# A scale's chain in the order of a scheduled kernel: higher priority, two steps fewer, and one block's features on ScalarE

## The chip, the cores and the metric

The kernel runs on one core of a Trainium2 chip. The metric is the device time of one execution in microseconds (us). The core's engines run side by side, each through its own list of instructions in order: TensorE (PE in the profile), VectorE (DVE), ScalarE (ACT), GpSimd (POOL) and SyncE (SP), which here issues most DMAs. An instruction that needs a result of another engine waits for it, and all that stands behind it on its engine waits too.

## The reference

One layer of a diffusion backbone: attention and mLSTM heads side by side, a projection, and a SwiGLU feed-forward net (FFN). The FFN is what matters here:

```python
def swiglu(h, w_gu, w_down):
    g, u = jnp.split(h @ w_gu, 2, axis=-1)
    return (jax.nn.silu(g) * u) @ w_down

h2 = rmsnorm(x, norm2_w) * (1 + sc2) + sh2      # the FFN's features
x = x + g2 * swiglu(h2, w_gu, w_down)
```

The width is 1024 and the hidden width 2816, which is 22 slices of 128 for each of gate and up. There are 9 blocks of 128 tokens, taken as three chunks (0, 1, 2) of three blocks. All inputs and outputs are fp32.

## The kernel before, in words

**Chunk 0** goes through the FFN in fp32 with split operands: a value is held as a rounded high part and a low part (L175 casts the high part on ACT, L146 subtracts it from the whole on DVE or POOL), and each product takes three matmuls, high by high, high by low and low by high (L1220 to L1222 in the down projection, L1481 to L1483 in gate and up). While a slice of w_gu passes, ACT sums its squares into a column of `wsum` (L179, 44 columns).

**Chunks 1 and 2** go through the FFN together in fp16 parts, in "stage six", which replaces eight block products by seven (`pair6`, twelve matmuls each, L1651 to L1653). `weights6` makes its weight operands: it loads raw tiles of w_gu (L1625), adds them (S, L1629 to L1632), and splits them into fp16 tiles A with ACT (L1637) and DVE (L1638). Both need one power of two for w_gu, `six[:, 2:3]`. `features6` makes the other operand `Bt`, from transposed rows: a multiply-add for each of eight pieces of a block (F, L1593 on ACT and L1595 on DVE), differences T of two chunks (L1609 to L1612), and their splits (L1600 and L1616 on ACT, L146 on DVE).

**The power of two** comes from `weight_scale`: DVE takes the largest of the 44 sums (L1548), PE transposes the column, DVE takes the maximum (`pv`, L201), halves the exponent by a shift and an add on the bits (L203, L204, since these are squares), bounds it from below (L191), keeps the exponent's bits (L192) and makes the scale and its inverse (L193, L194). PE spreads the two numbers over the partitions by a matmul with a row of ones (L208), and DVE copies them to `six` (L209). `power_scale` is used for other scales too.

**Crossing from chunk 0 to stage six.** Chunk 0's last group holds five slices. Its down projection has two halves of the columns, n = 0 and n = 1, each with three blocks of 15 matmuls of 128x512. DVE gates a finished block out of its bank (t, L1209) and adds it to the row (L1210). In n = 0, block 0 goes first and then blocks 1 and 2 interleaved; `weight_scale` is called at the third step of n = 0 (`scaled_down`), `weights6(0)` behind the first step of n = 1.

**The order on each engine** is not the order of the code: a scheduler with a simulated timeline picks the next instruction by readiness and priority. `hot(n)` raises the priority of what is issued in it; `features6` runs under `hot(600)`. In stage six each step also passes a slice of w_down, loaded and summed for a later scale (`down_tally`: a 512 KB load at L1559, absolute values on ACT at L1561), 22 in all.

Of the kernel before, what the change touches and what calls it, by code (L numbers as in the profile page):

```python
# [12 lines left out]
I32 = mybir.dt.int32  # L13
AF = mybir.ActivationFunctionType
ALU = mybir.AluOpType
AX = mybir.AxisListType
# [15 lines left out]
NF = D_FF // P  # L32
EPS = 1e-6
CB = 3
# [16 lines left out]
def hybrid_step(ctx: ExitStack, tc: tile.TileContext, I: dict, O: dict):  # L51
    nc = tc.nc
    mm = nc.tensor.matmul
    act = nc.scalar.activation
    dve = nc.vector
# [4 lines left out]
    def hot(n):  # L60
        return tc.high_priority(n)

    def nm(s):
        uid[0] += 1
        return f"{s}_{uid[0]}"
# [10 lines left out]
    def emit(gen):  # L76
        for _ in gen:
            pass
# [31 lines left out]
    def bank():  # L110
        turn_of[0] += 1
        at = psum["mm"] if "mm1" not in psum or turn_of[0] % 4 else psum["mm1"]
        return at.tile([P, 512], F32, name=nm("mm"), tag="mm")
# [10 lines left out]
    def transpose(out, in_, n=P):  # L124
        nc.tensor.transpose(out, in_, ident[:n, :n])
# [19 lines left out]
    def sub(out, full, hi, eng):  # L145
        (dve if eng == "dve" else pool).tensor_tensor(out=out, in0=full, in1=hi, op=ALU.subtract)  # L146
# [38 lines left out]
    def behind(key):  # L185
        return tc.issue_after(loaded[key]) if key in loaded else nullcontext()

    def powers(v, n):

        v = v[0:n]  # L190
        dve.tensor_scalar(out=v[:, 0:1], in0=v[:, 0:1], scalar1=2.0 ** -16, scalar2=None, op0=ALU.max)  # L191
        dve.tensor_scalar(out=v[:, 1:2].bitcast(I32), in0=v[:, 0:1].bitcast(I32), scalar1=0x7F800000, scalar2=None, op0=ALU.bitwise_and)  # L192
        dve.tensor_scalar(out=v[:, 2:3].bitcast(I32), in0=v[:, 1:2].bitcast(I32), scalar1=-1, scalar2=266 * 2 ** 23, op0=ALU.mult, op1=ALU.add)  # L193
        dve.tensor_scalar(out=v[:, 3:4], in0=v[:, 1:2], scalar1=2.0 ** -12, scalar2=None, op0=ALU.mult)  # L194

    def power_scale(tp, one, bound, out, squares=False):

        ps = bank()
        transpose(ps[0:1, 0:P], bound)
        v = tp.tile([1, 4], F32, name=nm("pv"), tag="pv", bufs=2)  # L200
        dve.tensor_reduce(out=v[:, 0:1], in_=ps[0:1, 0:P], axis=AX.X, op=ALU.max)  # L201
        if squares:
            dve.tensor_scalar(out=v[:, 1:2].bitcast(I32), in0=v[:, 0:1].bitcast(I32), scalar1=1, scalar2=None, op0=ALU.logical_shift_right)  # L203
            dve.tensor_scalar(out=v[:, 0:1].bitcast(I32), in0=v[:, 1:2].bitcast(I32), scalar1=1, scalar2=0x1FC00000, op0=ALU.mult, op1=ALU.add)  # L204
        powers(v, 1)
        yield
        ps = bank()
        mm(ps[:, 0:2], one, v[:, 2:4], start=True, stop=True)  # L208
        dve.tensor_copy(out, ps[:, 0:2])  # L209
        yield  # L210
# [150 lines left out]
    for n in (1, 4):  # L361
        dve.tensor_scalar(out=bcol[:, n * KD : (n + 1) * KD], in0=bcol[:, n * KD : (n + 1) * KD],
                          scalar1=1.0, scalar2=None, op0=ALU.add)
# [839 lines left out]
    def t2():  # L1203
        return ft.tile([P, 512], F32, name=nm("t2"), tag="t2", bufs=nt2[0])
# [303 lines left out]
    def down(c, a, f0, nf, n):  # L1508
        g = gate_bc(1, n)
        acts = a["act"]  # L1510
        pieces = []
        for j in range(0, nf, 2):
            m = min(2, nf - j)
            rows = w_down[(f0 + j) * P : (f0 + j + m) * P, n * 512 : (n + 1) * 512].rearrange("(a p) n -> p a n", p=P)
            pieces.append(load_piece([(full_view, rows)], (m, 512)))
        yield from three_blocks(
            lambda k, i: (acts[k][0][:, i * P : (i + 1) * P], acts[k][1][:, i * P : (i + 1) * P]),
            pieces, nf, lambda i, ps: add_gated(a["x1"][i], ps, g(c * CB + i), n))
# [26 lines left out]

    def weight_scale():

        dve.tensor_reduce(out=six[:, 7:8], in_=wsum[:, 0 : 2 * NF], axis=AX.X, op=ALU.max)  # L1548
        emit(power_scale(fp, ones, six[:, 7:8], six[:, 2:4], squares=True))
        dve.tensor_tensor(out=six[:, 4:5], in0=six[:, 1:2], in1=six[:, 3:4], op=ALU.mult)  # L1550
        dve.tensor_tensor(out=six[:, 6:7], in0=six[:, 4:5], in1=six[:, 4:5], op=ALU.mult)
        dve.tensor_scalar(out=six[:, 5:6], in0=six[:, 4:5], scalar1=0.5, scalar2=None, op0=ALU.mult)

    def down_tally(j):

        loaded["n"] = (loaded["n"] + 1) % len(piece_tags)
        tag = piece_tags[loaded["n"]]
        raw = homes.get(tag, wp).tile([P, D], F32, name=nm("whi"), tag=tag, bufs=2)
        dma(raw, w_down[j * P : (j + 1) * P, :])  # L1559
        jk = ft.tile([P, D], BF16, name=nm("jk"), tag="t2", bufs=nt2[0])  # L1560
        act(jk, raw, AF.Abs, accum_out=wsum[:, 2 * NF + j : 2 * NF + j + 1])  # L1561

    def tallies():

        for j in range(NF):
            down_tally(j)
            yield

    def down_scale():

        n = NF
        dve.tensor_reduce(out=six[:, 7:8], in_=wsum[:, 2 * NF : 2 * NF + n], axis=AX.X, op=ALU.max)
        emit(power_scale(up, ones, six[:, 7:8], six[:, 8:10]))
        dve.scalar_tensor_tensor(out=six[:, 10:11], in0=six[:, 6:7], scalar=1.0 / DOWN_C, in1=six[:, 9:10], op0=ALU.mult, op1=ALU.mult)

    def features6(a, c, i, Bt, firsts):

        x1, r = a["x1"][i], a["rs"][i]
        at = slice(i * P, (i + 1) * P)
        F = a4p.tile([P, KD, P], F32, name=nm("F"), tag="A4", bufs=7)  # L1580
        wide = psum["S"].tile([P, 3, 512], F32, name=nm("S"), tag="S") if i % 2 == 0 else None
        for half in range(2):
            with hot(600):
                y = t2()
                act(y, x1[:, half * 512 : (half + 1) * 512], AF.Copy, scale=r)
                ps = wide[:, half] if i % 2 == 0 else psum["po"].tile([P, 512], F32, name=nm("po"), tag="po")
                for j in range(4):
                    transpose(ps[:, j * P : (j + 1) * P], y[:, j * P : (j + 1) * P])
                for j in range(4):
                    k = half * 4 + j  # L1590
                    s, t = mods6[:, k, 0:1], mods6[:, k, 1:2]
                    if j == 0:
                        act(F[:, k], ps[:, j * P : (j + 1) * P], AF.Identity, scale=s, bias=t)  # L1593
                    else:
                        dve.tensor_scalar(out=F[:, k], in0=ps[:, j * P : (j + 1) * P], scalar1=s, scalar2=t, op0=ALU.mult, op1=ALU.add)  # L1595
            yield
        for half, b in ((0, B11), (1, B21)) if c == 1 else ((1, B22),):
            v = F[:, half * 4 : half * 4 + 4]
            with hot(600):
                nc.scalar.copy(Bt[:, b, 0, :, at], v)  # L1600
                sub(Bt[:, b, 1, :, at], v, Bt[:, b, 0, :, at], "dve")
            yield
        if c == 1:
            firsts.append(F)
            return
        first = firsts.pop(0)
        T = sp.tile([P, 4, 4, P], F32, name=nm("T"), tag="S", bufs=1)
        with hot(600):
            dve.tensor_tensor(out=T[:, T1], in0=first[:, 0:4], in1=F[:, 0:4], op=ALU.subtract)  # L1609
            dve.tensor_tensor(out=T[:, T2], in0=F[:, 4:8], in1=T[:, T1], op=ALU.add)  # L1610
            dve.tensor_tensor(out=T[:, T3], in0=F[:, 0:4], in1=F[:, 4:8], op=ALU.subtract)
            dve.tensor_tensor(out=T[:, T4], in0=first[:, 4:8], in1=T[:, T2], op=ALU.subtract)  # L1612
        yield
        for j in (0, 2):
            with hot(600):
                nc.scalar.copy(Bt[:, j : j + 2, 0, :, at], T[:, j : j + 2])  # L1616
                sub(Bt[:, j : j + 2, 1, :, at], T[:, j : j + 2], Bt[:, j : j + 2, 0, :, at], "dve")
            yield
# [200 lines left out]
    sx = ctx.enter_context(tc.tile_pool(name="sx", bufs=1, reuse_waits="tile"))  # L1819
    six = sx.tile([P, 12], F32, name="six")  # L1820
    wsum = sx.tile([P, 4 * NF], F32, name="wsum")
    mods6 = sx.tile([P, KD, 2], F32, name="mods6")
    ones = sx.tile([1, P], F32, name="ones")
    dve.memset(ones, 1.0)
# [55 lines left out]
    def late_rows():  # L1880
        rows_back(o_d[CB:], lambda: mixing(a4p, "A4", 7), late, 700)
        yield

    feats = chain(late_rows(), *[features6(nxt, 1, i, Bt, firsts) for i in range(CB)],
                  [None], attn_out(far, g_d[0, 1], late), *[features6(far, 2, i, Bt, firsts) for i in range(CB)])

    def scaled_down():
        for i, units in enumerate(down(0, cur, *GROUPS[-1], 0)):
            if i == 3:
                weight_scale()  # L1890
            yield units

    main = chain(groups(0, cur, GROUPS[NG:-1]), gate_up(cur, *GROUPS[-1]), scaled_down())
# [95 lines left out]
```

## Time and profile before

| | |
|---|---|
| three runs | 1494.35, 1494.94 (median), 3020.9 us |
| the profiled execution | 1496.35 us, of which the span of instructions is 1494.6 |
| PE busy | 1410.6 us, 94% of the span |
| DVE busy | 1103.5 us, 74% |
| ACT busy | 873.7 us, 58% |
| mean granted PE clock | 0.983 |

Times in the profile count from the start of its span. In rows of the timeline stand the start, the duration, the engine, the line, the operation with its tiles (out <- in), and in brackets the time for which the engine had been idle and what released it. Rows of the windows give, for a stretch, each engine's busy time (with instructions), the granted PE clock, the DMA engines' share and the rate. Matmul rows overlap, since the next starts before the last has drained.

### The profile page before, as it was taken

The page shows a single profiled execution, that of the slowest core. Times are in us where ns is not written, and L with a number is a line of the kernel's source. Part 1 is how long each engine was busy: PE and PEld are TensorE (multiplying, and loading weights), DVE is VectorE, ACT ScalarE, POOL GpSimd, SP SyncE. Part 2 cuts the span into 40 slices and gives each one's busy share as a digit, 9 for nine tenths or more (in the row PEclk, how much of TensorE's full clock was granted, in tenths as well). Part 3 has the DMA queues.
Part 4 walks back from the last instruction along what each step waited for, and adds up shares of the span by engine and source line. Part 5 has one row for each costly group of instructions (what it writes and reads, how often), then busy time and mean ns, then how long its engine had stood idle before and what let it go on. Part 6 is the DMA issues. An engine that isn't in the chain of part 4 may idle for free.

```text
span 1494.6 us, 22805 instructions
## 1 busy us (share of the span) xinstructions
PE 1410.6 (94%) x8285; PEld 989.5 (66%) x8285; DVE 1103.5 (74%) x2240; ACT 873.7 (58%) x1613; POOL 218.1 (15%) x310
## 2 busy tenths in 40 slices
PE   6899999998899889999999999998999999999996
PEld 3644667666677667888999997974645654654552
DVE  4878556775777988667687758788976877786667
ACT  4854477865857745464776754849642642463254
POOL 0113422232222435410100010000000000000000
PEclk9799999999999999999999999999999999999998
DMA  9565323753558865666757764459231321232112
GB/s 369 171 201 189 95 75 65 145 94 67 93 106 167 202 216 149 172 201 172 202 154 174 183 148 146 141 193 348 85 107 43 101 83 43 71 113 70 44 43 85
DMA packets 256166, 206.46 MB, mean 138 GB/s; under 512 B 167022, under 2 KB 208198, under 8 KB 256054
## 3 DMA queue, kind: packets, MB, share of 16 engines
q1 hardware_dynamic: 253054, 199.00, 47.9%
q10 hardware_dynamic: 2872, 5.62, 1.1%
q8 instruction: 65, 1.06, 0.3%
q14 instruction: 47, 0.39, 0.1%
q0 software_dynamic: 128, 0.39, 0.1%
HBM read 153.38 MB, written 13.26 MB: 111 GB/s over the span
## 4 chain that ended last, share of the span: by engine, by line
PE 54%; DVE 7%; DMA 3%; ACT 3%; issue 1%; POOL 0%; SPq 0%; ACTq 0%; DVEq 0%; POOLq 0%
PE mm L1653 6%; PE mm L1651 6%; PE mm L1652 6%; PE mm L1735 3%; PE mm L1736 3%; PE mm L1737 3%; PE mm L1482 3%; PE mm L1483 3%; PE mm L1481 3%; PE S L1132 2%; PE mm L1221 2%; PE mm L1220 2%; PE mm L1222 2%; PE mm L1256 2%; PE mm L1258 1%
## 5 line engine op out<-in xcount | busy, mean ns | idle before, releaser
L1651 PE MATMUL mm<-Bt,A 128*128 128x384 f16 x616 | 198.2, 326 | 2.8 <-ACT A L1637 1.3
L1652 PE MATMUL mm<-Bt,A 128*128 128x384 f16 x616 | 200.8, 326 | 0.0
L1653 PE MATMUL mm<-Bt,A 128*128 128x384 f16 x616 | 198.0, 326 | 1.7 <-DVE A L1638 1.7
L175 ACT CAST whi<-raw 128x1024 fp32r<-128x1024 f32 (+1 forms) x78 | 79.5, 1024 | 78.1 <-PE mm L1221 27.5
L1139 DVE SCALAR_TENSOR_TENSOR pl<-pr,st,ph 128x1152 f16<-128x1152 f32 (+1 forms) x72 | 97.9, 1360 | 36.6 <-ACT ph L1138 36.6
L146 DVE TENSOR_TENSOR wlo<-raw,whi 128x1024 fp32r<-128x1024 f32 (+1 forms) x78 | 93.3, 1197 | 41.6 <-ACT whi L175 37.8
L1481 PE MATMUL mm<-aTh,whi 128*128 128x384 f32 x352 | 119.2, 339 | 0.0
L1483 PE MATMUL mm<-aTh,wlo 128*128 128x384 f32 x352 | 119.0, 339 | 0.0
L1482 PE MATMUL mm<-aTl,whi 128*128 128x384 f32 x352 | 118.9, 338 | 0.0
L1135 ACT ACTIVATE pr<-S,st 128x1152 f32<-128x1152 f32 (+1 forms) x72 | 81.6, 1133 | 56.4 <-DVE st L1134 55.2
L1134 DVE TENSOR_REDUCE st<-S 128x1 f32<-128x1152 f32 (+1 forms) x72 | 88.9, 1234 | 25.2 <-PE S L1132 25.1
L530 PE MATMUL wi<-headw,hT 128*128 128x384 f16 x288 | 94.5, 328 | 1.2 <-ACT th L820 1.2
L531 PE MATMUL wi<-headw,hT 128*128 128x384 f16 x288 | 94.5, 328 | 0.0
L532 PE MATMUL wi<-headw,hT 128*128 128x384 f16 x288 | 94.4, 328 | 0.0
L1132 PE MATMUL S<-kst,qT 128*128 128x384 f32 (+1 forms) x400 | 87.6, 349 | 4.0 <-ACT pr L1135 4.0
L1138 ACT ACTIVATE ph<-pr,st 128x1152 f16<-128x1152 f32 (+1 forms) x72 | 83.7, 1163 | 12.7 <-DVE st L1137 5.3
L1651 PEld LDWEIGHTS <-A 128*128 128x128 f16 x616 | 60.2, 98 | 42.8 <-ACT A L1637 2.8
L1653 PEld LDWEIGHTS <-A 128*128 128x128 f16 x616 | 60.3, 98 | 42.2 <-DVE A L1638 2.5
L1652 PEld LDWEIGHTS <-A 128*128 128x128 f16 x616 | 60.3, 98 | 42.1 <-issue 2.6
L1132 PEld LDWEIGHTS S<-kst,qT 128*128 128x128 f32 x400 | 69.4, 189 | 7.8 <-ACT pr L1135 5.4
L146 POOL TENSOR_TENSOR hl<-tn,hl 128x384 fp32r<-128x384 f32 x22 | 28.9, 1314 | 313.2 <-ACT hl L1504 297.8
L1637 ACT ACTIVATE A<-S,six 128x1024 f16<-128x1024 f32 x44 | 49.0, 1141 | 37.3 <-PE mm L1653 19.7
(478 smaller groups left out, 3724.3 us busy)
## 6 DMA issues: line engine op xcount, KB each, us to landing
raw<-in_w_gu_dram SPq DMA_DIRECT2D x88, 512.0 KB, 3.6
raw<-in_w_down_dram SPq DMA_DIRECT2D x42, 512.0 KB, 3.9
a<-in_w_ada_dram SPq DMA_DIRECT2D x24, 512.0 KB, 6.4
whi<-in_w_down_dram SPq DMA_DIRECT2D x22, 512.0 KB, 8.6
iraw<-in_w_in_dram SPq DMA_DIRECT2D x32, 256.0 KB, 3.3
x<-in_x_sample_dram SPq DMA_DIRECT2D x11, 512.0 KB, 5.7
raw<-in_w_out_dram SPq DMA_DIRECT2D x10, 512.0 KB, 3.7
aw<-in_w_ada_dram SPq DMA_DIRECT2D x8, 512.0 KB, 5.4
```

Source lines behind the costliest of these rows:

```text
L146: (dve if eng == "dve" else pool).tensor_tensor(out=out, in0=full, in1=hi, op=ALU.subtract)
L530: mm(ps[:, :n], ah, wh[:, k % 2, c0 : c0 + n], start=(k == 0), stop=False)
L531: mm(ps[:, :n], ah, wl[:, k % 2, c0 : c0 + n], start=False, stop=False)
L532: mm(ps[:, :n], al, wh[:, k % 2, c0 : c0 + n], start=False, stop=(k == KD - 1))
L1132: mm(S[:, n, 0:w], qT[:, h, :], kst[kv][:, t, c0 + n * w : c0 + (n + 1) * w], start=(t == 0), stop=(t == 1))
L1139: dve.scalar_tensor_tensor(out=plv, in0=prv, scalar=st[:, 3:4], in1=phv, op0=ALU.mult, op1=ALU.subtract)
L1481: mm(ps, wh[:, k, :], th[:, k, :], start=(k == 0), stop=False)
L1482: mm(ps, wh[:, k, :], tl[:, k, :], start=False, stop=False)
L1483: mm(ps, wl[:, k, :], th[:, k, :], start=False, stop=(k == KD - 1))
L1651: mm(ps, wh[:, k], bt[:, 0, k], start=first and k == 0, stop=False, skip_group_check=True)
L1652: mm(ps, wh[:, k], bt[:, 1, k], start=False, stop=False, skip_group_check=True)
L1653: mm(ps, wl[:, k], bt[:, 0, k], start=False, stop=k == 3, skip_group_check=True)
```

## The change

1. `weight_scale()` is called under `hot(900)`.
2. For squares, the shift and the add on bits become one multiply-add: 0.5 times the number that the bits form, plus 0x1FC00000. The lower bound L191 is left out for this call; a constant column of 2^-32 in `wsum` takes its place, which is set at the start, so that w_down's columns move by one. The chain has five DVE steps from `pv` to the scale instead of seven.
3. In `features6`, all eight multiply-adds of the last block of chunk 2 go to ACT; before, two of the eight did.

```diff
-    def powers(v, n):
+    def powers(v, n, least=True):
         v = v[0:n]
-        dve.tensor_scalar(out=v[:, 0:1], in0=v[:, 0:1], scalar1=2.0 ** -16, scalar2=None, op0=ALU.max)
+        if least:
+            dve.tensor_scalar(out=v[:, 0:1], in0=v[:, 0:1], scalar1=2.0 ** -16, scalar2=None, op0=ALU.max)
...
         if squares:
-            dve.tensor_scalar(out=v[:, 1:2].bitcast(I32), in0=v[:, 0:1].bitcast(I32), scalar1=1, scalar2=None, op0=ALU.logical_shift_right)
-            dve.tensor_scalar(out=v[:, 0:1].bitcast(I32), in0=v[:, 1:2].bitcast(I32), scalar1=1, scalar2=0x1FC00000, op0=ALU.mult, op1=ALU.add)
-        powers(v, 1)
+            dve.tensor_scalar(out=v[:, 0:1].bitcast(I32), in0=v[:, 0:1].bitcast(I32), scalar1=0.5, scalar2=0x1FC00000, op0=ALU.mult, op1=ALU.add)
+        powers(v, 1, not squares)
...
     def weight_scale():
-        dve.tensor_reduce(out=six[:, 7:8], in_=wsum[:, 0 : 2 * NF], axis=AX.X, op=ALU.max)
+        dve.tensor_reduce(out=six[:, 7:8], in_=wsum[:, 0 : 2 * NF + 1], axis=AX.X, op=ALU.max)
...
-                    if j == 0:
+                    if j == 0 or (c, i) == (2, CB - 1):
                         act(F[:, k], ps[:, j * P : (j + 1) * P], AF.Identity, scale=s, bias=t)
...
+    dve.memset(wsum[:, 2 * NF : 2 * NF + 1], 2.0 ** -32)
...
             if i == 3:
-                weight_scale()
+                with hot(900):
+                    weight_scale()
```

In the order of the changed kernel, lines from L192 to L204 of before stand one lower in number (L193 for L192 and so on; its L204 is the new multiply-add).

**VectorE, at the end of half n = 0.** Before, from the second gating of n = 0 to the end of the chain (`pv`):

```order
L1209 TENSOR_TENSOR t_2204_11204<-mm_11155,gl_8050 128x512
L1209 TENSOR_TENSOR t_2205_11207<-mm_11156,gl_8050 128x512
L1612 TENSOR_TENSOR T_11100<-F_10317,T_11100 128x512
L191 TENSOR_SCALAR pv_11172<-pv_11172 1x1
L1210 TENSOR_TENSOR x1a<-x1a,t_2198_11152 128x512
L146 TENSOR_TENSOR Bt<-T_11100,Bt 128x2x4x128
L1210 TENSOR_TENSOR x1a<-x1a,t_2204_11204 128x512
L1210 TENSOR_TENSOR x1a<-x1a,t_2205_11207 128x512
L192 TENSOR_SCALAR pv_11172<-pv_11172 1x1
L146 TENSOR_TENSOR Bt<-T_11100,Bt 128x2x4x128
L193 TENSOR_SCALAR pv_11172<-pv_11172 1x1
L194 TENSOR_SCALAR pv_11172<-pv_11172 1x1
```

And the same place after the change, from the new multiply-add on:

```order
L204 TENSOR_SCALAR pv_11173<-pv_11173 1x1
L146 TENSOR_TENSOR wlo_11225<-raw_11223,whi_11224 128x512
L1612 TENSOR_TENSOR T_11101<-F_10318,T_11101 128x512
L193 TENSOR_SCALAR pv_11173<-pv_11173 1x1
L146 TENSOR_TENSOR Bt<-T_11101,Bt 128x2x4x128
L194 TENSOR_SCALAR pv_11173<-pv_11173 1x1
L195 TENSOR_SCALAR pv_11173<-pv_11173 1x1
L1209 TENSOR_TENSOR t_2198_11153<-mm_11133,gx_11113 128x512
L1209 TENSOR_TENSOR t_2204_11203<-mm_11156,gl_8051 128x512
L1209 TENSOR_TENSOR t_2205_11206<-mm_11157,gl_8051 128x512
L146 TENSOR_TENSOR Bt<-T_11101,Bt 128x2x4x128
L209 COPY six<-mm_11179 128x2
```

The whole chain now stands ahead of the three gatings of n = 0, with one large Bt subtraction in front of its end and the other behind the gatings.

**TensorE, between the halves.** Before, L208 stands behind the first block of n = 1 (mm_11270), which itself follows the last matmul of n = 0:

```order
L1222 MATMUL mm_11270<-whi_11219,hl_11019 128x512
L1220 MATMUL mm_11270<-whi_11225,hl_11109 128x512
L1221 MATMUL mm_11270<-wlo_11226,hl_11109 128x512
L1222 MATMUL mm_11270<-whi_11225,hl_11109 128x512
L208 MATMUL mm_11180<-pv_11172,ones 128x2
L1220 MATMUL mm_11230<-whi_11213,hl_10743 128x512
L1221 MATMUL mm_11230<-wlo_11214,hl_10743 128x512
```

After, it follows the last matmul of n = 0 (mm_11133, mm_11156, mm_11157 are that half's blocks):

```order
L1222 MATMUL mm_11133<-whi_11128,hl_11110 128x512
L1222 MATMUL mm_11156<-whi_11128,hl_11110 128x512
L1222 MATMUL mm_11157<-whi_11128,hl_11110 128x512
L208 MATMUL mm_11179<-pv_11173,ones 128x2
L1220 MATMUL mm_11229<-whi_11212,hl_10744 128x512
L1221 MATMUL mm_11229<-wlo_11213,hl_10744 128x512
L1222 MATMUL mm_11229<-whi_11212,hl_10744 128x512
```

All 45 matmuls of n = 1 now stand behind L208; before, 15 of them stood ahead of it.

**SyncE, the loads at the start of stage six.** Before (raw_11481 and raw_11483 are the weights of slice 1 of stage six, raw_11678 belongs to slice 2; whi are slices of w_down to be summed):

```order
L1525 DMA fw_11520<-in_final_norm_w_dram 128x512
L1625 DMA raw_11678<-in_w_gu_dram 128x1024
L1525 DMA fw_11522<-in_final_norm_w_dram 128x512
L1559 DMA whi_11393<-in_w_down_dram 128x1024
L1559 DMA whi_11477<-in_w_down_dram 128x1024
L1625 DMA raw_11481<-in_w_gu_dram 128x1024
L1625 DMA raw_11483<-in_w_gu_dram 128x1024
L1559 DMA whi_11413<-in_w_down_dram 128x1024
```

After:

```order
L1525 DMA fw_11519<-in_final_norm_w_dram 128x512
L1559 DMA whi_11392<-in_w_down_dram 128x1024
L1559 DMA whi_11476<-in_w_down_dram 128x1024
L1525 DMA fw_11521<-in_final_norm_w_dram 128x512
L1625 DMA raw_11480<-in_w_gu_dram 128x1024
L1625 DMA raw_11482<-in_w_gu_dram 128x1024
L1625 DMA raw_11677<-in_w_gu_dram 128x1024
L1559 DMA whi_11412<-in_w_down_dram 128x1024
```

The two slices of w_down now stand ahead of every raw weight tile listed here, and slice 1's tiles ahead of slice 2's first one. On ScalarE the eight features of the last block stand in groups of four, three and one (before, single ones in two places), all of them ahead of the 128x512 cast of the last weight piece of n = 1 (L175), as the two did before. GpSimd's list is the same in both kernels, and the order on the other engines up to some 20 us before this place too, apart from the new memset.

More of the change, by code (lines that the diff above doesn't have):

```diff
@@ L1560, in down_tally @@
         jk = ft.tile([P, D], BF16, name=nm("jk"), tag="t2", bufs=nt2[0])
-        act(jk, raw, AF.Abs, accum_out=wsum[:, 2 * NF + j : 2 * NF + j + 1])
+        act(jk, raw, AF.Abs, accum_out=wsum[:, 2 * NF + 1 + j : 2 * NF + j + 2])
     def tallies():
@@ L1571, in down_scale @@
         n = NF
-        dve.tensor_reduce(out=six[:, 7:8], in_=wsum[:, 2 * NF : 2 * NF + n], axis=AX.X, op=ALU.max)
+        dve.tensor_reduce(out=six[:, 7:8], in_=wsum[:, 2 * NF + 1 : 2 * NF + 1 + n], axis=AX.X, op=ALU.max)
         emit(power_scale(up, ones, six[:, 7:8], six[:, 8:10]))
```

## The prediction

> **What bounds the kernel now.** The page's first part shows the engine with most work, and a window query cuts the end of the run into stretches. Columns of a window: PE, its weight loads, DVE, ACT and POOL busy (instructions), granted PE clock, DMA share, GB/s.
>
> ```profile
> PE 1410.6 (94%) x8285; PEld 989.5 (66%) x8285; DVE 1103.5 (74%) x2240; ACT 873.7 (58%) x1613; POOL 218.1 (15%) x310
> 974.00:996.00 22.00, 19.34 (x91) 15.71 (x90) 21.30 (x41) 8.35 (x12) 2.47 (x1) 1.00 0.54 198
> 996.00:1002.40 6.40, 6.40 (x29) 5.02 (x27) 6.17 (x13) 5.11 (x6) 0.00 (x0) 1.00 0.44 116
> 1002.40:1036.00 33.60, 29.10 (x171) 16.03 (x171) 25.55 (x48) 28.31 (x48) 0.00 (x0) 1.00 0.98 367
> 1036.00:1475.00 439.00, 438.99 (x2450) 239.60 (x2449) 327.04 (x496) 198.48 (x256) 0.00 (x0) 1.00 0.23 76
> ```
>
> PE is the engine that sets the time. From 1036 to 1475 it has no gap (438.99 of 439.00), so whatever is won ahead of 1036 reaches the end as it is, and nothing that another engine does in those 439 us can give it back or add to it, short of opening a gap. Where the change acts, PE idles twice: 2.66 us in 974 to 996 (22.00 less 19.34) and 4.50 us in 1002.4 to 1036. In the first of these DVE is full (21.30 of 22.00) and ACT is not (8.35); in the second DMA is full (0.98). At most 2.66 + 4.50 = 7.16 us are to be had.
>
> The timeline of PE shows the single gaps: the first two in the crossing, the others in the first 33 us of stage six.
>
> ```profile
> 987.76 0.86 PE L1222 MATMUL mm<-whi,hl 128*128 128x512 f32 x3
> 990.14 0.50 PE L1220 MATMUL mm<-whi,hl 128*128 128x512 f32 x1 [1.51 <-DVE t L1209]
> 995.05 0.38 PE L208 MATMUL mm<-pv,ones 1*128 1x2 f32 x2 [1.15 <-DVE pv L194]
> 995.36 0.50 PE L1220 MATMUL mm<-whi,hl 128*128 128x512 f32 x1
> 1002.44 0.34 PE L1651 MATMUL mm<-Bt,A 128*128 128x384 f16 x1
> 1014.80 0.32 PE L1651 MATMUL mm<-Bt,A 128*128 128x384 f16 x1 [0.40 <-DVE u L1670]
> 1020.26 0.34 PE L1653 MATMUL mm<-Bt,A 128*128 128x384 f16 x1 [0.82 <-DVE A L1638]
> 1027.65 0.34 PE L1653 MATMUL mm<-Bt,A 128*128 128x384 f16 x1 [0.90 <-DVE A L1638]
> 1034.86 0.32 PE L1651 MATMUL mm<-Bt,A 128*128 128x384 f16 x1 [0.67 <-DVE u L1670]
> ```
>
> Half n = 0 ends at 988.62 (987.76 + 0.86). PE then waits 1.51 us for a bank that DVE gates out, and 1.15 us for the scale chain's last step.
>
> **The change, part by part.** DVE's timeline through the crossing:
>
> ```profile
> 983.05 1.04 DVE L1595 TENSOR_SCALAR F<-S,mods 128x128 f32<-128x128 f32 x3
> 984.01 0.27 DVE L201 TENSOR_REDUCE pv<-mm 1x1 f32<-1x128 f32 x1
> 985.41 0.13 DVE L203 TENSOR_SCALAR pv<-pv 1x1 int32<-1x1 int32 x1
> 985.59 0.69 DVE L146 TENSOR_TENSOR wlo<-raw,whi 128x512 fp32r<-128x512 f32 x1
> 988.20 0.69 DVE L1209 TENSOR_TENSOR t<-mm,gx 128x512 f32<-128x512 f32 x1 [0.66 <-PE mm L1222]
> 988.80 1.28 DVE L1209 TENSOR_TENSOR t<-mm,gl 128x512 f32<-128x512 f32 x2
> 990.00 0.68 DVE L1612 TENSOR_TENSOR T<-F,T 128x512 f32<-128x512 f32 x1
> 993.60 0.13 DVE L192 TENSOR_SCALAR pv<-pv 1x1 int32<-1x1 int32 x1
> 993.67 1.20 DVE L146 TENSOR_TENSOR Bt<-T,Bt 128x1024 f16<-128x1024 f32 x1
> 994.86 0.13 DVE L194 TENSOR_SCALAR pv<-pv 1x1 f32<-1x1 f32 x1
> 996.12 0.14 DVE L209 COPY six<-mm 128x2 f32<-128x2 f32 x1
> ```
>
> *The priority.* The chain ends at 994.99 (994.86 + 0.13), because it stands behind three gatings, T, three sums of rows and two Bt subtractions. In the new order five DVE rows end it, behind `wlo` 128x512. From one start to the next the rows above give 0.60 for a pass of 128x512 (988.20 to 988.80; I take it for `wlo` and T too), 0.07 for a small step (993.60 to 993.67), and 1.19 for Bt with L193 behind it (993.67 to 994.86). If `wlo` starts at 985.59 as before, the scale is ready at 985.59 + 0.60 + 0.60 + 0.07 + 1.12 (Bt without L193) + 0.07 + 0.13 = 988.18, which is 6.8 us earlier, and 0.44 us ahead of PE's end of n = 0. L208 then starts at 988.62 without a wait.
>
> *Whether `wlo` keeps its start.* DVE has ahead of it the same rows as before, less six features, plus one Bt 128x512 and one T (0.60 each, as above) that the new order moves there. Three features take 0.96 (983.05 to 984.01), so the sum is -1.92 + 1.20 = -0.72. `wlo` cannot use that, since its cast on ACT sets it:
>
> ```profile
> 980.40 0.46 ACT L1593 ACTIVATE F<-S,mods 128x128 f32<-128x128 f32 x1
> 980.90 0.51 ACT L1504 CAST hl<-tn 128x384 fp32r<-128x384 f32 x1
> 984.93 0.62 ACT L175 CAST whi<-raw 128x512 fp32r<-128x512 f32 x1 [3.52 <-PE mm L1221]
> 996.30 1.15 ACT L1637 ACTIVATE A<-raw,six 128x1024 f16<-128x1024 f32 x1 [4.54 <-DVE six L209]
> L1593 ACT ACTIVATE F<-S,mods x8: 451/455/459, 892.2 to 980.4; 128x128 f32<-128x128 f32 x8
> L1595 DVE TENSOR_SCALAR F<-S,mods x24: 396/401/410, 893.0 to 983.7; 128x128 f32<-128x128 f32 x24
> ```
>
> ACT waited 3.52 us there for PE to free the piece. Cast end 985.55, `wlo` 985.59: unchanged, if ACT is not late.
>
> *The six features on ACT.* Six at 0.455 are 2.7 us at most, some 2.1 us if they overlap like DVE's (0.40 long, 0.32 apart). ACT also takes one cast of F (L1600) ahead of the 984.93 place now, 0.62 us if it is as long as the cast of the same size above. 2.1 to 2.7 + 0.6 stands against 3.52 us of idling, so 0.2 to 0.8 us are left, and I cost it at nothing. The cast of `hl` that n = 0's last slice needs (980.90) slips by one to two us; PE first reads it with the ninth matmul from the end of n = 0 (by the order; 9 x 0.236 us, from the 30 below), at about 986.5, so that is hidden too. Without this cover each microsecond would go to PE. If part 3 were left out, DVE would be 1.92 - 0.72 = 1.20 us late at `wlo`, and L208 0.8 us late.
>
> The Trainium skill, page "ScalarE: Activation LUTs", section "Rules for kernel authors", says to put adds and multiplies on VectorE and not on ScalarE. This trace agrees on the single instruction (0.401 against 0.455 us); going by the rule one would leave the six on DVE and the kernel 0.8 us worse by the sum above, since what counts here is the engine that is full.
>
> *Two steps less.* Each is 0.07 us where it fills DVE's queue back to back and up to 0.18 where the next step waits (985.41 to 985.59). L203 and L191 together are 0.14 to 0.36 us on DVE, which lie inside the slack of `wlo`; alone they give 0 to 0.3 us. I take 0. The memset is one small step long before; 0.
>
> *The first wait of n = 1.* Before, its first block waited for the end of the third gating (990.08; PE resumed at 990.14). Now the first matmul needs a bank that the first gating frees. That gating comes behind the chain at 988.2, as before, since block 0's last matmul sets it, and ends at 988.89. L208 occupies PE to 988.93 (0.31 from 995.05 to 995.36). So n = 1 starts at about 989.0, and its 45 matmuls follow without a wait: 30 of them took 7.08 us (995.36 to 1002.44), so 45 take 10.62. Stage six starts at 999.6 instead of 1002.44: a gain of 2.8, which I bound by the two gaps, **2.66**. It shrinks if the scale is late; the ends are 1.5 and 2.7.
>
> *Stage six's first 33 us.* The other gain comes from what waits for `six`. L209 moves from 996.12 to about 991.2 (988.2 + 1.8 for three gatings + 1.12 for a Bt), 4.9 us. ACT, which sat idle 4.54 us for it, can make slice 0's A tiles that much earlier, which frees the raw buffers for slice 1's loads. SP's and ACT's rows there:
>
> ```profile
> 1000.29 0.85 SPq L1559 DMA_DIRECT2D whi<-in_w_down_dram  x2
> 1001.69 1.11 SPq L1625 DMA_DIRECT2D raw<-in_w_gu_dram  x2
> 1008.95 1.15 ACT L1637 ACTIVATE A<-raw,six 128x1024 f16<-128x1024 f32 x1 [1.43 <-DMA raw<-in_w_gu_dram]
> 1011.50 1.06 ACT L1561 ACTIVATE jk<-whi 128x1024 bf16<-128x1024 f32 x1 [1.04 <-DMA whi<-in_w_down_dram]
> ```
>
> Slice 1's loads were issued at 1001.69. By the order they can go about 3.4 us earlier, when slice 0's last A is made, and run in the stretch 996 to 1002.4 where DMA was at 0.44. The chain of loads, sums and A tiles would then run 3.4 to 4.9 us earlier while PE needs it 2.7 us earlier: 0.7 to 2.2 us of lead. The gaps quoted are 0.40 to 0.90 us each, and all add to 4.50; a lead of that size covers one after another, but they are serial, and each one taken away makes PE arrive earlier at the next, so the lead is spent on them. Lead of 0.7 gives 0.7 us, lead of 4.5 would give all. The sums (22 at about 1.0 us on ACT) also come earlier, which unloads ACT later in the stretch. The ends are 0 and 4.5; I take **3.5**, nearer to the upper end, because ACT idled 2.47 us in this chain for loads alone (1.43 + 1.04), which earlier issues fill.
>
> Sum: 2.7 + 3.5 = 6.2 us. The profiled execution took 1496.35, so it would take 1490.2, with a span of 1488.4. It lies 1.4 above the median of 1494.94; from the median, **1488.8**.
>
> **The rivals.**
>
> *A. Only the crossing.* The 4.5 us stay, because that stretch moves 367 GB/s at a DMA share of 0.98: a stage bound by bytes shifts as a whole. For it: two slices of w_down now stand ahead of slice 1's raw tiles and of the others, 2 x 0.524 MB, at 367 GB/s 2.9 us, near the lead. Against it: they stood ahead of slice 1's tiles before too (1000.29), and the stretch ahead has free DMA. Gain 1.5 to 3.2, time 1491.7 to 1493.4. The Trainium skill, page "DMA: Bandwidth & Descriptors", section "Queues, rings and completion order", has each queue row and engine as one ring of its own; the rows above agree with loads that are served in the order of issue, as the raw tiles issued behind two slices were in use 7.3 us after their issue.
>
> *B. Nothing moves.* The chain's end is not what PE really waits for, or another DVE row takes its place; then n = 1 waits for gating as before. Gain 0 to 1.5, time 1493.4 to 1495. DVE is full to 97% there, which speaks for it; that six features leave it speaks against.
>
> *C. Slower.* L208 now heads a queue of 45 matmuls, where 15 used to hide it. It needs L194's successor, that needs `wlo`, that needs ACT's cast, behind all eight features, the second four of which need PE's transposes first. If ACT reaches the cast d us after 984.93, L208 is d - 0.4 late and PE stands still for it. From d = 3.1 on, the 2.7 us are used up and the kernel is slower; at d = 5, by 1.9 us, if stage six gives nothing back: 1495 to 1498. ACT has 3.52 us of idling ahead of that, so d = 3.1 takes 6.6 us of extra work, twice what I find.
>
> **How the numbers follow.** Forecast (gain 4.5 to 7.2) 0.60; A 0.23; B 0.10; C 0.07. The forecast's own range is 1487.5 to 1490.5, with 1 us of noise below (the three times and the profiled one differ by up to 2). The range takes in the forecast and A: 1486.3 to 1493.7. A change of 2% would be 29.9 us, and is about what a measurement of this kernel can tell from no change; all cases lie within it, so faster by more 0.01, within 0.97, slower by more 0.02.
>
> **What would show it.** In the profile after: L208 right behind the last L1222 of n = 0 with no idle time; the first L1220 of n = 1 at about 989 with under 0.4 us of idling; the 128x512 cast on ACT still released by PE at about 984.9; stage six's first L1651 at about 999.7; L209 near 991; slice 1's raw loads near 998.3; under 1.5 us of PE gaps in the 33 us that follow, and none behind. It would be wrong if the cast on ACT is late, if L208 waits for `pv`, or if the gaps in stage six only move by 2.7 us with the rest.

## The result, and the profile after

The changed kernel takes 1492.59 us (median of 9 runs) against 1496.5 for the kernel before in the same job; the ratio is 0.9971, with a 95% interval of 0.996 to 0.9982. By the ratio that is 4.3 us less, between 2.7 and 6.0: no change by the bound of 2%, but clear of the spread. The ratios, here and below, leave out single slow runs, which the medians count: 1748.61 us after, at a granted clock of 0.785, 3020.9 before, and one each of no_priority and no_features. The profiled execution took 1491.52 with a span of 1489.8, 4.8 under the span before.

The windows after the change, with the columns as before:

```profile
974.00:996.00 22.00, 21.99 (x102) 17.99 (x102) 21.99 (x39) 9.76 (x14) 2.98 (x1) 1.00 0.48 181
996.00:1002.40 6.40, 6.40 (x36) 4.25 (x35) 5.48 (x9) 5.69 (x8) 0.00 (x0) 1.00 0.91 229
1002.40:1036.00 33.60, 31.41 (x191) 18.09 (x189) 27.11 (x52) 29.18 (x51) 0.00 (x0) 1.00 0.98 366
1036.00:1470.00 434.00, 432.42 (x2407) 235.29 (x2406) 322.33 (x489) 194.86 (x251) 0.00 (x0) 1.00 0.23 75
```

PE no longer idles in 974 to 996 (19.34 us busy before, 21.99 now). The DMA engines fill the next 6.4 us (0.44 before, 0.91 now), and the stretch behind is as full as it was (0.98, 366 GB/s), with 2.2 us of idling left, and 1.6 us more behind 1036, where there was none.

The timeline of PE, in the crossing and at the gaps that are left:

```profile
986.95 0.86 PE L1222 MATMUL mm<-whi,hl 128*128 128x512 f32 x3
987.74 0.38 PE L208 MATMUL mm<-pv,ones 1*128 1x2 f32 x2
988.13 0.50 PE L1220 MATMUL mm<-whi,hl 128*128 128x512 f32 x1
998.70 0.34 PE L1651 MATMUL mm<-Bt,A 128*128 128x384 f16 x1
...
1009.23 0.34 PE L1653 MATMUL mm<-Bt,A 128*128 128x384 f16 x1 [0.28 <-DVE A L1638]
1016.30 0.34 PE L1653 MATMUL mm<-Bt,A 128*128 128x384 f16 x1 [0.82 <-DVE A L1638]
1023.42 0.34 PE L1653 MATMUL mm<-Bt,A 128*128 128x384 f16 x1 [1.10 <-DVE A L1638]
1042.32 0.32 PE L1651 MATMUL mm<-Bt,A 128*128 128x384 f16 x1 [1.20 <-DVE u L1670]
```

L208 and the first matmul of n = 1 carry no idle time. In stage six four gaps of 3.40 us in all stand here, and one of 0.26 later (1216.46); before it was eight, of 4.40 us.

Absolute times differ between executions by a few us from what lies ahead, so what follows goes by two stretches of one trace: the **crossing**, from the last matmul of gate and up (L1483) to stage six's first (L1651), and **stage six**, from its first L1651 to its last. Both come from the rows by line, whose pair of times is the first and the last start. Before:

```profile
L1483 PE MATMUL mm<-aTh,wlo x352: 333/336/445, 629.3 to 977.3; 128*128 128x384 f32 x176
L1651 PE MATMUL mm<-Bt,A x616: 322/326/337, 1002.4 to 1451.8; 128*128 128x384 f16 x154
```

After:

```profile
L1483 PE MATMUL mm<-aTh,wlo x352: 333/336/442, 630.6 to 976.8; 128*128 128x384 f32 x176
L1651 PE MATMUL mm<-Bt,A x616: 322/326/337, 998.7 to 1446.9; 128*128 128x384 f16 x154
```

The crossing went from 25.1 to 21.9 us (-3.2), stage six from 449.4 to 448.2 (**-1.2**). But 0.3 of the 3.2 us is only where the crossing begins. Four transposes for the features (S, L125) stand inside it in the kernel before:

```profile
977.09 0.34 PE L1482 MATMUL mm<-aTl,whi 128*128 128x384 f32 x1
979.76 0.60 PE L125 MATMUL S<-ident,t 128*128 128x128 f32 x4
```

After the change they stand ahead of the last L1483, so outside it:

```profile
976.25 0.34 PE L1482 MATMUL mm<-aTl,whi 128*128 128x384 f32 x1
976.42 0.60 PE L125 MATMUL S<-ident,t 128*128 128x128 f32 x4
```

From the last L1482, which has the transposes behind it in both, stage six starts 25.35 us later before and 22.45 after (**-2.9**). Together that is 4.1 us of the span's 4.8; of the rest, 0.8 lies ahead of the last L1482 and is counted to the spread, and 0.1 was lost behind stage six.

### The profile page after: what moved, and what is told of

Its sections match the earlier page's. It is cut to its first block, busy times and chain, and to the rows that moved or that the text cites. A ratio compares the mean times of both kernels' runs of the same rounds, so it can differ in the third digit from the quotient of the medians.

```text
span 1489.8 us, 22801 instructions
## 1 busy us (share of the span) xinstructions
PE 1406.6 (94%) x8285; PEld 986.0 (66%) x8285; DVE 1102.7 (74%) x2233; ACT 875.8 (59%) x1619; POOL 218.7 (15%) x310
## 3 DMA queue, kind: packets, MB, share of 16 engines
q8 instruction: 65, 1.06, 0.3%
## 4 chain that ended last, share of the span: by engine, by line
PE 51%; DVE 6%; DMA 5%; ACT 4%; issue 2%; POOL 1%; SPq 0%; ACTq 0%; DVEq 0%; POOLq 0%
PE mm L1651 5%; PE mm L1653 5%; PE mm L1652 5%; PE mm L1482 3%; PE mm L1481 3%; PE mm L1483 3%; PE mm L1735 3%; PE mm L1736 3%; PE mm L1737 3%; PE mm L1220 2%; PE S L1132 2%; PE mm L1221 2%; PE mm L1222 2%; PE mm L1256 1%; PE mm L1258 1%
## 5 line engine op out<-in xcount | busy, mean ns | idle before, releaser
L1651 PE MATMUL mm<-Bt,A 128*128 128x384 f16 x616 | 198.4, 326 | 1.5 <-DVE u L1670 1.2
L146 DVE TENSOR_TENSOR wlo<-raw,whi 128x1024 fp32r<-128x1024 f32 (+1 forms) x78 | 95.1, 1221 | 38.6 <-ACT whi L175 35.2
L175 ACT CAST whi<-raw 128x1024 fp32r<-128x1024 f32 (+1 forms) x78 | 79.7, 1027 | 70.7 <-PE mm L1221 26.2
L1483 PE MATMUL mm<-aTh,wlo 128*128 128x384 f32 x352 | 119.1, 339 | 0.5 <-DVE wlo L146 0.5
L1482 PE MATMUL mm<-aTl,whi 128*128 128x384 f32 x352 | 118.9, 338 | 0.0
L1651 PEld LDWEIGHTS <-A 128*128 128x128 f16 x616 | 60.3, 98 | 40.4 <-ACT A L1637 0.4
```

The lines of the kernel that those rows point to most:

```text
L1482: mm(ps, wh[:, k, :], tl[:, k, :], start=False, stop=False)
L1483: mm(ps, wl[:, k, :], th[:, k, :], start=False, stop=(k == KD - 1))
L1651: mm(ps, wh[:, k], bt[:, 0, k], start=first and k == 0, stop=False, skip_group_check=True)
```

## The experiments

All in one table: the two stretches (the crossing also from the last L1482, which compares kernels with and without part 3 fairly), the sum of the gaps that PE's timeline of stage six records, and the time against the kernel before.

| kernel | crossing | from L1482 | stage six | gaps | median us | ratio [95%] |
|---|---|---|---|---|---|---|
| before | 25.1 | 25.35 | 449.4 | 4.40 | | |
| after | 21.9 | 22.45 | 448.2 | 3.66 | 1492.59 | 0.9971 [0.996, 0.9982] |
| after_again | 21.9 | 22.46 | 448.4 | 3.70 | 1490.76 | 0.9961 [0.9949, 0.9973] |
| no_priority | 22.0 | 22.44 | 449.8 | 4.97 | 1493.81 | 0.9964 [0.9945, 0.9982] |
| no_features | 23.9 | 24.13 | 450.5 | 5.82 | 1496.75 | 0.9992 [0.9978, 1.0006] |
| features_only | 23.9 | 24.41 | 452.0 | 6.87 | 1497.07 | 0.9998 [0.9983, 1.0013] |
| half_pace | 22.1 | 22.69 | 450.8 | 4.84 | 1491.66 | 0.9959 [0.9944, 0.9974] |
| short_sums | 22.0 | 22.48 | 448.8 | 4.67 | 1493.38 | 0.9971 [0.9961, 0.9982] |
| short_loads | 21.9 | 22.45 | 448.0 | 3.05 | 1492.08 | 0.9959 [0.9946, 0.9972] |
| short_both | 22.1 | 22.68 | 446.3 | 2.30 | 1488.17 | 0.9951 [0.9934, 0.9968] |
| late_sums | 22.0 | 22.46 | 446.2 | 2.58 | 1490.84 | 0.9964 [0.9948, 0.9979] |
| late_sums_again | 21.9 | 22.46 | 447.3 | 3.44 | 1491.13 | 0.9959 [0.9944, 0.9973] |
| late_finish | 22.0 | 22.45 | 453.6 | 7.65 | 1497.79 | 1.0008 [0.9995, 1.002] |

### Which part moved the chain

**The priority.** The edit takes back part 1.

```diff
-                with hot(900):
-                    weight_scale()
+                weight_scale()
```

> The changed kernel with weight_scale called without the raised priority; parts 2 and 3 stay. Theory R (the priority does nothing, the two other parts moved the chain; its order is that of the changed kernel row for row on all engines): crossing without a gap, L208 right behind n = 0, PE gaps in stage six about 3.4 us as after, time within 0.1% of the changed kernel's 1492.6. Theory P (the raised priority moves the chain, as the prediction priced it): 1.5 and 1.15 us of gaps back, some 2.7 us or more slower than the changed kernel.

The crossing is 22.0 us, as after, without theory P's gaps. The order explains it: each engine's instructions stand in the same order as after, row for row but for a branch's line number. The same holds the other way round: `hot(900)` alone in the kernel before leaves its order as it was (that one was not run, since it is the same program), and so it does in no_features and features_only below. The priority did nothing here. The gaps in stage six were 4.97 us in this execution against 3.66, although the order is the same. Of the difference 0.61 us lies in the first 45 us, where slice 1's first A waits 2.85 us for its load instead of the 2.08 after the change; the other 0.70 lies at 1218 to 1221 behind VectorE's u and c, and no run shows its cause.

**The features.** The edit takes back part 3.

```diff
-                    if j == 0 or (c, i) == (2, CB - 1):
+                    if j == 0:
```

> The changed kernel without part 3: the six features stay on VectorE. The chain then ends behind the three gatings and L1612, and L208 stands behind the first block of n = 1. Theory R2 (both parts are needed for the whole gain): the wait for the third gating is back, about 1.5 us, L208 waits for nothing (1.15 us kept); L209 some 1 to 2 us earlier than before; time 1.2 to 2.5 us under before. Theory of the prediction (VectorE late by 1.2 us, L208 still at the head of n = 1 and 0.8 us late): gap of 0.8 us at L208 and none ahead of n = 1.

PE's gaps in the crossing and at the start of stage six:

```profile
987.25 0.50 PE L1220 MATMUL mm<-whi,hl 128*128 128x512 f32 x1 [1.51 <-DVE t L1209]
1007.71 0.32 PE L1651 MATMUL mm<-Bt,A 128*128 128x384 f16 x1 [1.41 <-ACT p L1660]
```

Since the priority moves nothing, this is part 2 alone. The wait for the third gating is back with the same 1.51 us as before, the one at L208 is not, and the crossing keeps 1.2 of its 2.9 us. Theory R2 had this, and the prediction's L208 at the head of n = 1 is refuted. But stage six gives 1.1 us back, at a place where before there was no gap: a copy of ScalarE (p, L1660) that stands behind slice 1's first A tile, which waits for its load:

```profile
1003.59 1.06 ACT L1561 ACTIVATE jk<-whi 128x1024 bf16<-128x1024 f32 x1 [3.87 <-DMA whi<-in_w_down_dram]
1006.15 1.15 ACT L1637 ACTIVATE A<-raw,six 128x1024 f16<-128x1024 f32 x1 [1.41 <-DMA raw<-in_w_gu_dram]
```

That A starts 7.8 us after stage six did (998.33); before it was 6.5 (1008.95 against 1002.44), after 6.0. Its load was issued 0.30 us ahead of stage six's start (998.03), against 0.75 before (1001.69). So here a crossing that is shorter, without loads that come earlier by as much, wins nothing that the time shows: 1.2 us by the ratio, between 3.3 less and 0.9 more, where R2 had 1.2 to 2.5.

**The features alone.** The edit makes part 3 in the kernel before.

```diff
-                    if j == 0:
+                    if j == 0 or (c, i) == (2, CB - 1):
```

> The kernel before with part 3 alone: six features of the last block go to ScalarE, the chain keeps seven steps. In its order five of the seven steps still end behind the gatings, and L208 stands behind the first block of n = 1. Theory R2: the wait for the third gating stays, about 1.5 us, L208 waits for nothing (chain's end near 993.1, L208 near 993.7), gain of 1.15 us in the crossing, 1 to 2.5 us in all. Rival (the features are the whole of it): both gaps gone, as fast as the changed kernel, 4 us under before.

```profile
990.59 0.50 PE L1220 MATMUL mm<-whi,hl 128*128 128x512 f32 x1 [1.77 <-DVE t L1209]
1010.91 0.32 PE L1651 MATMUL mm<-Bt,A 128*128 128x384 f16 x1 [1.28 <-ACT p L1660]
```

PE's timeline shows the same picture: a crossing 0.9 us shorter than before from the last L1482, the same new gap behind p, 2.6 us lost in stage six, and no gain in time. I had given it 1 to 2.5 us. Neither part 2 nor part 3 changes the time measurably by itself (the intervals leave room for 3.3 and 2.5 us less); only with both does the scheduler find the chain done ahead of the end of n = 0, put L208 in front of all of n = 1 and the chain in front of the gatings.

The Trainium skill's rule on page "ScalarE: Activation LUTs", section "Rules for kernel authors" (adds and multiplies belong on VectorE) would have kept the six features on VectorE: that is no_features, with a crossing 1.7 us longer than after (24.13 against 22.45). The rule is about an instruction, and holds for it; here VectorE was the full engine and ScalarE had 2.99 us of waiting left even after it took them.

### Where the rest of the gain in stage six went

What is compared is bytes (B) against ScalarE's list (Q), with VectorE's own work (D) as a third. ScalarE in the changed kernel:

```profile
996.71 2.19 ACT L1637 ACTIVATE A<-S,six 128x1024 f16<-128x1024 f32 x2 [5.05 <-DVE S L1632]
...
1004.72 1.15 ACT L1637 ACTIVATE A<-raw,six 128x1024 f16<-128x1024 f32 x1 [2.08 <-DMA raw<-in_w_gu_dram]
1005.78 0.46 ACT L1660 COPY p<-mm 128x384 f32<-128x384 f32 x1
1008.58 1.06 ACT L1561 ACTIVATE jk<-whi 128x1024 bf16<-128x1024 f32 x1 [2.34 <-DMA whi<-in_w_down_dram]
...
1013.80 2.17 ACT L1637 ACTIVATE A<-S,six 128x1024 f16<-128x1024 f32 x2
```

And SyncE's issue of slice 1's two loads (and slice 2's first):

```profile
997.38 1.52 SPq L1625 DMA_DIRECT2D raw<-in_w_gu_dram  x3
```

Slice 1's loads were issued at 997.38, 4.3 us earlier than before, and its first A starts 4.2 us earlier. The next sum starts only 2.9 us earlier (1011.50 before): it waits 2.34 us for its slice of w_down. Behind it four sums, a square and then the A tiles for which PE waits at 1016.30. Those come 15.1 us after stage six's start, and 15.3 before (1017.75 against 1002.44): the lead was gone, and the gap is the same 0.82 us as at 1020.26 before.

Most of the lead was never there. Slice 1's tiles take the places of weight pieces of chunk 0, so in both orders the last thing that their loads wait for is the matmuls of n = 1 that read these pieces, and not ScalarE's A tiles of slice 0. SyncE's waits from 989 to 1003 (us in total, times, longest), before:

```profile
SPq L1625 <- PE mm L1222: 1.2, 2, 0.7
```

After; the first row is the w_down slice ahead of slice 1's tiles:

```profile
SPq L1559 <- PE mm L1222: 5.7, 1, 5.7
SPq L1625 <- PE mm L1222: 0.3, 1, 0.3
```

So the loads move with PE itself: they were issued 0.75 us ahead of stage six's start before (1001.69 against 1002.44) and 1.32 ahead after (997.38 against 998.70), a lead of 0.6 us. Nor did the earlier scale bring all of slice 0's A tiles earlier. The first came 5.8 us earlier (996.30 to 990.51), but the next two only 0.9 (997.62 to 996.71), since ScalarE then waited 5.05 us for VectorE's sums S.

**Half the pace.** Slices of w_down at every second step.

```diff
-            for _ in pair6(f, Bt, acts):
+            for step, _ in enumerate(pair6(f, Bt, acts)):
...
-                next(to_tally, None)
+                if step % 2 == 0:
+                    next(to_tally, None)
```

> The changed kernel with the 22 slices of w_down loaded and summed at every second step of stage six instead of every step, so over slices 0 to 4 instead of 0 to 2. Theory S (the 3.4 us of PE gaps in the first 45 us of stage six come from loads and sums of w_down, by bytes or by ScalarE's order): gaps under 1 us, 2.5 to 3.4 us faster than the changed kernel, about 1489.7. Rival D (VectorE's own work, S and low parts of A, sets them): gaps stay at about 3.4 us, time as the changed kernel's. Rival L (the later scale of w_down comes late): a new gap of 1 us or more behind slice 4, and no gain.

The first gaps stay and PE's timeline has a new one:

```profile
1006.64 0.34 PE L1653 MATMUL mm<-Bt,A 128*128 128x384 f16 x1 [0.51 <-DVE A L1638]
1013.72 0.34 PE L1653 MATMUL mm<-Bt,A 128*128 128x384 f16 x1 [0.82 <-DVE A L1638]
1022.15 0.32 PE L1651 MATMUL mm<-Bt,A 128*128 128x384 f16 x1 [2.41 <-ACT p L1660]
```

The scheduler still puts three sums ahead of slice 1's A and six loads next to its tiles, so the start is no better; the edit did not do what I meant by it. The gaps of the first 45 us add to 3.74 us, which is what rival D had given, but as the start kept its loads and sums this does not decide against S. Rival L's gap behind slice 4 did not come.

**Short sums, short loads, and both.** The edits, for short_sums the second pair of lines, for short_loads the first with the sum stretched over the quarter four times, for short_both both pairs:

```diff
-        dma(raw, w_down[j * P : (j + 1) * P, :])
+        dma(raw[:, :256], w_down[j * P : (j + 1) * P, :256])
...
-        act(jk, raw, AF.Abs, accum_out=wsum[:, 2 * NF + 1 + j : 2 * NF + j + 2])
+        act(jk[:, :256], raw[:, :256], AF.Abs, accum_out=wsum[:, 2 * NF + 1 + j : 2 * NF + j + 2])
```

> The changed kernel; the 22 slices of w_down are loaded whole, but ScalarE sums only a quarter of each (256 of 1024 columns), so their scale is not the right one. Theory Q (ScalarE's list: a weight tile A stands behind four or five sums of 1.04 us each, so shorter sums bring A about 3 us earlier): the gaps that wait for A or p go, PE gaps in stage six under 1 us, 2.5 us faster than the changed kernel from the start of stage six to its end. Theory B (bytes: 11.5 MB of slices ahead of the weight tiles at some 400 GB/s): gaps stay at 3 us or more, since the loads land as before.

> The changed kernel; of each of the 22 slices of w_down a quarter is loaded (256 columns), and ScalarE sums that quarter four times over, so that its work stays as long (their scale is not the right one). Theory B: the loads no longer hold up the weight tiles, the two waits of ScalarE for loads (2.08 and 2.34 us after the change) go, A tiles 2 to 4 us earlier, gaps under 1 us. Theory Q: ScalarE's first sums come up to 4 us earlier too, but it stays full for longer, and gaps of 1.5 us or more remain where A and p stand behind sums.

> The changed kernel with a quarter of each slice loaded and a quarter summed: neither bytes nor ScalarE's sums are left as a limit. Both theories: gaps in the first 45 us of stage six under 0.5 us, stage six 3.5 us shorter. If VectorE's own work set them (theory D), 2 us or more would remain.

ScalarE with short sums, where A's second group should have come 3 us earlier:

```profile
1005.87 1.15 ACT L1637 ACTIVATE A<-raw,six 128x1024 f16<-128x1024 f32 x1 [4.28 <-DMA raw<-in_w_gu_dram]
1009.72 0.42 ACT L1561 ACTIVATE jk<-whi 128x256 bf16<-128x256 f32 x1 [2.34 <-DMA whi<-in_w_down_dram]
1014.86 2.18 ACT L1637 ACTIVATE A<-S,six 128x1024 f16<-128x1024 f32 x2
```

ScalarE with short loads:

```profile
1004.56 1.14 ACT L1637 ACTIVATE A<-raw,six 128x1024 f16<-128x1024 f32 x1
1005.60 0.46 ACT L1660 COPY p<-mm 128x384 f32<-128x384 f32 x1
1012.22 2.18 ACT L1637 ACTIVATE A<-S,six 128x1024 f16<-128x1024 f32 x2
```

And all of PE's gaps in stage six of that kernel:

```profile
1031.28 0.34 PE L1653 MATMUL mm<-Bt,A 128*128 128x384 f16 x1 [0.79 <-DVE A L1638]
1071.85 0.58 PE L208 MATMUL mm<-pv,ones 1*128 1x2 f32 x2 [2.26 <-DVE pv L195]
```

With a quarter of the bytes and sums of full length, both waits for loads are gone, the second group comes 12.1 us after stage six's start instead of 15.1, and one gap of 0.79 us is left in the first 45 us. With all the bytes and sums of 0.42 us, the waits for loads stay (2.34 as after, and 4.28 instead of 2.08, since the sums ahead are done 1.0 us sooner and the tile is used 8.1 us after its issue instead of 7.3), the second group comes at 15.9, and the gaps are 4.67 us. That is B's picture. Two limits: with short sums the scheduler put three squares of 1.04 us ahead of that group where one stood after, so ScalarE's list was not as much shorter as meant, and Q as an addition to B isn't excluded. With short loads there were two squares ahead of it, and the group came earlier all the same. And stage six as a whole gained only 0.2 us with short loads, because a new gap of 2.26 us came at L208 of the next scale (w_down's, the chain of L195) at 1071.85. With both short, stage six is 1.9 us shorter than after, where 3.5 was expected, and the first 45 us hold 0.62 us of gaps, against 0.5 expected. Theory D asked for 2 us or more there, with VectorE's work as it was; it is refuted as the main cause.

By the Trainium skill, page "DMA: Bandwidth & Descriptors", section "Queues, rings and completion order", SyncE's queue row has one ring on each of the 16 engines and each ring is taken in order, so the tiles stand behind the slices that SyncE issued ahead of them, though by the same section loads need not complete in that order. The runs agree with the outcome: from issue to first use slice 1's tile takes 7.3 us (997.38 to 1004.72), and 3.9 us with short loads and sums (997.18 to 1001.12), where ScalarE came to it without a wait; they do not show the rings.

**Later sums.** The slices of w_down from slice 1 on, all loaded and summed whole.

```diff
-                next(to_tally, None)
+                if f > 0:
+                    next(to_tally, None)
```

> The changed kernel; the 22 slices of w_down start with slice 1 of stage six instead of slice 0, at the same pace of one a step. Theory B: slice 1's weight tiles have the queue to themselves and land 3 to 4 us earlier, the wait at its first A goes, and what follows meets the slices of w_down later with the lead of one slice: gaps under 2 us. Theory Q: sums stand ahead of slice 2's tiles as they stood ahead of slice 1's, and the same 3 to 4 us of gaps come 14 us later.

> The same kernel as late_sums, timed in the same job as the changed kernel: if its gain of some 2 us from the start of the crossing to the end holds, it is 0.1 to 0.2% under the changed kernel here.

> The changed kernel once more, for its spread: crossing 21.9 us from the last gate and up matmul to stage six (25.1 before) if the order sets it, and gaps in stage six of 3 to 5 us, which depend on when loads land; 0.3% under the kernel before.

Stage six is 2.0 us shorter than after in the first execution and 0.9 to 1.1 in the second, and the first A comes 5.1 and 5.7 us after its start. This edit, too, did less than was meant. Two slices of w_down are still issued right ahead of slice 1's tiles (at 993.63 against 995.71), and two instead of four right behind them. So the tile was in use 0.4 to 1.0 us earlier, not 3 to 4, and the wait for it fell only from 2.08 to 1.29 and 1.89 us. The gaps of the first 45 us are 1.87 and 2.47 us: B's "under 2" held once in two, and Q's 3 to 4 us at a later place came in neither. What is left is one larger gap; on VectorE, the row ahead of the low parts:

```profile
1010.62 4.07 DVE L1531 SCALAR_TENSOR_TENSOR x1a<-x1a,ry,fw 128x512 f32<-128x512 f32 x6
1014.60 2.48 DVE L1638 SCALAR_TENSOR_TENSOR A<-S,six,A 128x1024 f16<-128x1024 f32 x2
```

PE waits 1.71 us behind the six passes of chunk 0's last norm. In time it is not to be told from the changed kernel: 1491.13 against 1490.76 in the same job, 0.9959 [0.9944, 0.9973] against 0.9961 [0.9949, 0.9973]. So I have no version that is shown to beat the changed one.

**Later norm.** Late sums, and that norm from slice 4 on.

```diff
-                if f > 0:
+                if f > 3:
                     next(done6, None)
```

> The changed kernel with the 22 slices of w_down from slice 1 of stage six on (as in late_sums) and the last norm of chunk 0 (its squares on ScalarE, six passes of 4.06 us on VectorE at L1531, three stores) from slice 4 on instead of slice 1. Theory B with F (what is left of the gaps in late_sums, 1.71 us at one place, is the block of six passes ahead of A's low part): gaps in the first 45 us under 1 us, stage six under 446 us from its first to its last product, time 1 to 2 us under late_sums. Rival: the block only meets other work at slice 4, and the gap comes there.

It lost. The 1.71 us are gone, but 2.46 us of gaps are left in the first 45 us, where under 1 was expected. Stage six takes 453.6 us, 6.3 more than late_sums_again, of which the gaps explain 4.2, and the largest gap is, as in short_loads, L208 of w_down's scale:

```profile
1079.67 0.38 PE L208 MATMUL mm<-pv,ones 1*128 1x2 f32 x2 [3.71 <-DVE pv L195]
```

## Why the prediction was right or wrong

The time, 1492.59, lies in the range of 1486.3 to 1493.7, and it went the way that was forecast, but above the forecast's own 1487.5 to 1490.5 and where rival A had put it (1491.7 to 1493.4). The gain was 4.3 us where 6.2 was forecast. The times mislead here: the forecast was taken from a median of 1494.94 before, which is 1496.5 in this job. So 1.6 of the 3.8 us above 1488.8 are the base, and rival A's time was met by luck: its gain of at most 3.2 is further from 4.3 than the forecast's least, 4.5. The interval of 2.7 to 6.0 excludes neither.

The timelines of ScalarE and VectorE in the changed kernel, for the first points:

```profile
984.12 0.62 ACT L175 CAST whi<-raw 128x512 fp32r<-128x512 f32 x1 [2.99 <-PE mm L1221]
```

```profile
984.72 0.13 DVE L204 TENSOR_SCALAR pv<-pv 1x1 int32<-1x1 int32 x1
984.78 0.68 DVE L146 TENSOR_TENSOR wlo<-raw,whi 128x512 fp32r<-128x512 f32 x1
987.25 0.13 DVE L195 TENSOR_SCALAR pv<-pv 1x1 f32<-1x1 f32 x1
987.38 0.69 DVE L1209 TENSOR_TENSOR t<-mm,gx 128x512 f32<-128x512 f32 x1
990.32 0.15 DVE L209 COPY six<-mm 128x2 f32<-128x2 f32 x1
```

- *The scale's time*: right. It ends at 987.38, 0.43 us ahead of PE's end of n = 0 (986.95 + 0.86 = 987.81); 0.44 was forecast. L208 starts without a wait.
- *The cast on ScalarE sets `wlo`*: right. The cast starts at 984.12, still released by PE, after 2.99 us of waiting (3.52 before); `wlo` follows at 984.78.
- *What moved it*: wrong. I put the earlier chain down to the priority and the features as cover for it. The priority changes no row; parts 2 and 3 together do, and I had costed part 2 at nothing. Nor would leaving out part 3 have left L208 at the head of n = 1 and 0.8 us late: the scheduler moves L208 back behind a block when the chain comes later. The change's parts can't be priced on a fixed order where a scheduler decides it.
- *The crossing*: 2.66 forecast, 2.9 measured (from the last three matmuls of n = 0 to stage six 14.68 us before, 11.75 after). I took the gaps as they are recorded. A matmul's record reaches beyond the start of the next (three that start some 0.23 us apart are recorded as 0.86 us before a wait, so the last one as 0.40), so each interruption costs some 0.15 us more than its idle time.
- *Stage six*: the step that failed. 3.5 us were forecast, 1.2 came. The times of the chain came out: L209 4.9 us earlier forecast, 5.8 measured in absolute times; slice 1's loads at 998.3 forecast, 997.38 measured. The path did not. I let ScalarE's A tiles of slice 0 free the buffers for these loads; they wait for PE's own matmuls of n = 1, so they came 4.3 us earlier and PE 3.7, a lead of 0.6 us. That is near the 0.7 at the lower end of my own lead of 0.7 to 2.2, and by my own rule it is worth about what came (the gaps fell by 0.74 us). The 3.5 stood above that lead, on the ground that earlier issues fill ScalarE's waits for loads. They did not: those waits were 2.54 (at 1006.37, a row that I had left out), 1.43 and 1.04 us before, and are 2.08 and 2.34 after. The loads queue as before (366 GB/s over the stretch, 367 before), and the sum behind slice 1's first tile came only 2.9 us earlier. Of the gaps, "under 1.5 us" was forecast for stage six's first 33 us and 2.20 came; "none behind" was wrong by 1.46 (1.20 at 1042.32 and 0.26).
- *Rivals*: A named what keeps the gaps, as far as short_loads shows it; its own crossing, 1.5 to 3.2, was right, and stage six gave 1.2 instead of nothing. B is refuted by L208. C didn't occur; what a late cast would cost, no run shows.

What stays open: how much of the gaps is ScalarE's list rather than bytes (short_sums changed the order too), and what makes stage six differ by 1.6 us between two executions of one order (448.2 and 449.8), of which the gaps are 1.31.

## What to carry to other kernels

Look at the order before you price a priority: here it moved no instruction, and two parts that gained nothing measurable alone moved the chain together. Look up what a load really waits for before you give it a lead: here it was the engine that the lead was meant for. In this kernel, a gap closed ahead of the stage that loads at full rate was kept only as far as the loads came earlier by as much; measure the time from the stage's start to its first tiles (6.5, 6.0 and 7.8 us here), not the time of issue. Compare traces by stretches between two of their own rows, since what lies ahead shifts whole executions by more than the change is worth (the last L1483 starts at 973.7 to 982.7 us in the 13 traces), and see that the same work stands between these rows.

## What the runs showed of the hardware

Idle times as recorded understate an interruption of TensorE: two gaps of 2.66 us in all were worth 2.9. A 512 KB load among others took 7.3 us from issue to first use, and at most 3.9 where the slices of w_down beside it were a quarter as long. A short sum has a fixed part: 0.42 us for 256 columns, 1.06 for 1024, which leaves some 0.2 us that don't shrink with the columns (an estimate from the two).
